# A two-block network in float32: how the second block's weights get their low parts, and how the FFN's products are grouped

## The chip, the cores and the metric

The kernel runs on one core of a Trainium2 chip. The metric is the device time of one execution in microseconds, as the median of the runs. One execution of the kernel before was profiled; all rows below are from it.

## The reference

Two blocks follow each other on 256 positions of 1024 features, all in float32. The first block has two layers, each a mixer (a chunked recurrence, then attention) and a convolutional FFN. The second block has two layers of its own. Cut to what the change touches:

```python
def conv_ffn(x, norm_g, w_up, conv_w, conv_b, w_down):      # first block, D_FF = 2816
    u = rmsnorm(x, norm_g) @ w_up
    ...                                                      # causal convolution of 3 taps
    val, gate = jnp.split(c, 2, axis=-1)
    return (jax.nn.silu(gate) * val) @ w_down

def conformer_conv(u_val, u_gate, conv_w, conv_b, ln_g, ln_b, w_pw2):
    a = u_val * jax.nn.sigmoid(u_gate)                       # the gated unit
    y = lax.conv_general_dilated(a, ...) + conv_b            # 31 taps
    y = jax.nn.silu(layernorm(y, ln_g, ln_b))
    return y @ w_pw2

def second_block(x, c, ...):
    for l in range(DEPTH):
        ...
        h = rmsnorm_2(x, g_pre[l]) * (1.0 + scale[:, None, :]) + shift[:, None, :]
        p = h @ w_in[l]
        u_val, u_gate, g_conv, c_q, c_kv, k_idx, w_idx, g_attn = jnp.split(p, offsets, axis=-1)
        y_conv = conformer_conv(u_val, u_gate, ...) * jax.nn.silu(g_conv)
        y_attn = dsa_attention(c_q, c_kv, k_idx, w_idx, ...) * jax.nn.silu(g_attn)   # scores, top-64, softmax
        y = jnp.concatenate([y_conv, y_attn], axis=-1) @ w_out[l]
        x = x + gate[:, None, :] * rmsnorm_2(y, g_post[l])
```

## The kernel before

TensorE (PE) multiplies in two ways. A plain float32 product runs as two recorded halves. A *split* product (`mm3`) writes each operand as a rounded high part plus a low part and adds three rounded products: high by high, high by low, low by high. Nearly all weights are split: SP (the sync engine's queue) loads a part of up to 1024 columns (512 KB) into a float32 page, ScalarE (ACT) copies it rounded into a page of type R (`act(hi, raw)`, line 437), and VectorE (DVE) subtracts (`tt(lo, raw, hi)`, line 450). `split_w` does this, `Chunk` calls it for each part of a weight. Weights whose name is in `NATIVE` skip it and are multiplied in float32, straight from the loaded page: in each layer of the second block the last fourth of the gated unit's weights (`u3`), half of the two gates' (`w_ga1`, `w_gc1`), and the four parts of `w_out` that take the attention's output (`oa`).

Memory is a pool of pages of 1024 columns: 24 of type R, 25 of float32 (F), cut into quarters where a tile is small, and 8 PSUM banks. The order of all instructions on the five engines is set before the run by a planner: every operation has a priority, which is its place in the program as written, an assumed duration, and for transfers an assumed `tail` until they land. Each engine takes the ready operation of lowest priority for which pages are free. `pg.spread` moves a group's priorities to a given stretch of the program, so the 120 taps of the convolution (`CONV0, CONV1 = 0.8, 1.0`) and the steps of top-k.

The FFN (`ffn`) runs over 22 values of j. `up(j)` makes two blocks of 128 features by 256 positions: 8 values of k, three rounded products of 256 columns each, both blocks in one bank. ACT and DVE put the three taps on, reading the bank, and `down(j)` adds the result's product with `w_down`. In between, DVE reduces 48 tiles of `w_ada` (128 x 1024, `stt` with an accumulator), which the second block needs. The last six `down` chunks come at the end of an FFN, and in the second FFN they are ordered by quarters of the output, each of which runs through all six chunks.

A layer of the second block (`dsa_layer`) multiplies the scaled features with `w_lat` (48 products of 456 columns, 128 tokens after the other 128), normalizes, makes the index scores on 8 heads, finds the 64 highest of each row by 8 rounds of a maximum and a replacement on DVE, and then multiplies the gated unit's weights `w_u`, whose results the taps read. Queries, gates, masked softmax of 8 heads, `w_out`'s attention half, the convolution's end and `w_out`'s other half follow.

## Time and profile before

| | us |
|---|---|
| median of 3 runs | 865.4 |
| lowest, highest | 864.19, 865.57 |
| profiled execution | 863.71 |
| its span, first to last instruction | 861.9 |
| PE busy in it | 851.7 |
| DVE busy | 725.4 |
| ACT busy | 557.1 |

How to read it: the span is what the trace covers, the execution's own time is 1.8 us longer. A busy share is an average over stages that differ, so the rows below give it by stage too. The recorded length of a matmul covers its way through the array and overlaps the next one; what a product costs is the distance from its start to the next start. The granted clock of PE is 0.99 to 1.00 of full speed in every stretch shown. The first block's mixer takes the span up to about 125 us, its first FFN the stretch to 310, the attention mixer that to 430, the second FFN that to about 610, and the two layers of the second block the rest.

### The profile page before, as it was taken

What the parts mean: (1) busy time and instruction counts of PE and PEld (TensorE: products, weight loads), DVE (VectorE), ACT (ScalarE), POOL (GpSimd) and SP (SyncE); (2) the same over time, 40 slices, a digit from 0 to 9 for tenths busy, and PEclk for the clock granted to TensorE, in tenths of its full rate; (3) what the DMA queues carried; (4) which work ended last, traced back from release to release, by engine and by line L of the source; (5) the groups of instructions that cost most, each with busy time, mean ns of one, the idle gap of its engine ahead of it and who ended that gap; (6) DMA issues with size and microseconds to landing.
All of it is one profiled execution on the core that took longest, in us unless ns stands there. A gap on an engine that the chain in (4) does not pass through costs nothing.

```text
span 861.9 us, 15745 instructions
## 1 busy us (share of the span) xinstructions
PE 851.7 (99%) x5822; PEld 776.8 (90%) x5822; DVE 725.4 (84%) x1632; ACT 557.1 (65%) x1154; POOL 0.2 (0%) x4
## 2 busy tenths in 40 slices
PE   8999999999999999999999999999999999999997
PEld 7988999999999988889989999998999857998866
DVE  6766999999977699986999976675799998799895
ACT  7856587555555496774776655566952797953883
POOL 0000000000000000000000000000000000000000
PEclk9999999999999999999999999999999999999999
DMA  8995857988865353487479975632430167440201
GB/s 318 408 354 198 285 182 225 317 294 314 303 222 180 105 182 137 146 282 264 141 229 367 351 259 177 192 118 88 155 124 14 34 213 303 138 147 14 74 1 49
DMA packets 50412, 170.27 MB, mean 198 GB/s; under 512 B 5860, under 2 KB 8436, under 8 KB 50336
## 3 DMA queue, kind: packets, MB, share of 16 engines
q1 hardware_dynamic: 50192, 169.28, 56.8%
q8 instruction: 45, 0.74, 0.3%
q14 instruction: 31, 0.25, 0.1%
q10 hardware_dynamic: 144, 0.00, 0.0%
HBM read 167.89 MB, written 1.37 MB: 196 GB/s over the span
## 4 chain that ended last, share of the span: by engine, by line
PE 95%; DVE 2%; ACT 1%; DMA 1%; issue 0%; SPq 0%; DVEq 0%; ACTq 0%
PE ps L571 26%; PE ps L573 26%; PE ps L572 26%; PE ps L424 13%; PE ps L428 2%; DVE R L450 1%; DVE F L455 1%; PE ps L582 1%; DMA F<-in_x_dram 1%; ACT F L437 0%; ACT R L437 0%; DVE F L450 0%; PE ps L1247 0%; SPq L488 0%; ACT s L437 0%
## 5 line engine op out<-in xcount | busy, mean ns | idle before, releaser
L571 PE MATMUL ps<-R,R 128*128 128x256 f32 (+2 forms) x1644 | 505.0, 307 | 1.0 <-ACT R L437 1.0
L572 PE MATMUL ps<-R,R 128*128 128x256 f32 (+2 forms) x1644 | 496.4, 302 | 1.3 <-DVE R L450 1.2
L573 PE MATMUL ps<-R,R 128*128 128x256 f32 (+2 forms) x1644 | 496.0, 302 | 0.0
L450 DVE TENSOR_TENSOR R<-F,R 128x1024 fp32r<-128x1024 f32 (+4 forms) x339 | 324.1, 986 | 43.3 <-ACT R L437 31.7
L571 PEld LDWEIGHTS ps<-R,R 128*128 128x128 f32 x1644 | 314.1, 191 | 14.8 <-ACT R L437 2.2
L572 PEld LDWEIGHTS ps<-R,R 128*128 128x128 f32 x1644 | 314.1, 191 | 12.9 <-DVE R L450 2.7
L573 PEld LDWEIGHTS ps<-R,R 128*128 128x128 f32 x1644 | 313.8, 191 | 11.8 <-DVE R L450 0.6
L437 ACT ACTIVATE R<-F 128x1024 fp32r<-128x1024 f32 (+4 forms) x339 | 282.4, 864 | 32.0 <-DVE F L450 24.5
L424 PE MATMUL ps<-F,F 128*128 128x256 f32 (+6 forms) x576 | 128.0, 375 | 0.8 <-ACT F L437 0.7
L437 ACT ACTIVATE F<-ps 128x256 f32<-128x256 f32 (+4 forms) x189 | 69.5, 399 | 69.2 <-PE ps L573 39.6
L424 PEld LDWEIGHTS ps<-F,F 128*128 128x128 f32 (+2 forms) x576 | 90.9, 190 | 19.8 <-issue 8.2
L437 ACT ACTIVATE F<-ps,par 128x256 f32<-128x256 f32 (+1 forms) x84 | 42.3, 552 | 89.0 <-PE ps L573 88.7
L455 DVE SCALAR_TENSOR_TENSOR F<-ps,par,F 128x255 f32<-128x255 f32 (+1 forms) x160 | 66.1, 476 | 27.1 <-ACT F L437 26.9
L455 DVE SCALAR_TENSOR_TENSOR F<-F,par,F 128x256 f32<-128x256 f32 (+30 forms) x206 | 86.8, 466 | 1.4 <-ACT F L437 1.3
L455 DVE SCALAR_TENSOR_TENSOR F<-F,F 128x1024 f32<-128x1024 f32 (+1 forms) x53 | 60.2, 1146 | 6.7 <-ACT F L437 6.7
L437 ACT ACTIVATE F<-F 128x256 f32<-128x256 f32 (+2 forms) x112 | 43.9, 413 | 31.7 <-DVE F L455 16.0
L450 DVE TENSOR_TENSOR F<-ps,F 128x256 f32<-128x256 f32 (+2 forms) x72 | 29.7, 443 | 18.5 <-PE ps L573 16.1
L437 ACT ACTIVATE F<-F,s 128x128 f32<-128x128 f32 (+1 forms) x80 | 33.3, 444 | 3.4 <-DVE s L476 3.0
L437 ACT ACTIVATE R<-F,par 128x256 fp32r<-128x256 f32 x32 | 14.3, 504 | 30.0 <-DVE F L450 30.0
L455 DVE SCALAR_TENSOR_TENSOR F<-F,par 128x255 f32<-128x255 f32 (+14 forms) x66 | 30.8, 467 | 0.0
L1373 ACT ACT_TABLE_LOAD x23 | 29.5, 1283 | 0.4
L428 PEld LDWEIGHTS ps<-con,F 128*128 128x128 f32 (+2 forms) x158 | 19.7, 140 | 8.9 <-issue 2.8
(96 smaller groups left out, 365.2 us busy)
## 6 DMA issues: line engine op xcount, KB each, us to landing
F<-in_f_w_up_dram SPq DMA_DIRECT2D x88, 512.0 KB, 5.5
F<-in_w_ada_dram SPq DMA_DIRECT2D x48, 512.0 KB, 5.6
F<-in_f_w_down_dram SPq DMA_DIRECT2D x44, 512.0 KB, 5.4
F<-in_w_u_dram SPq DMA_DIRECT2D x16, 512.0 KB, 5.5
F<-in_w_out_dram SPq DMA_DIRECT2D x16, 512.0 KB, 3.7
F<-in_a_w_o_dram SPq DMA_DIRECT2D x8, 512.0 KB, 10.2
F<-in_a_w_out_dram SPq DMA_DIRECT2D x8, 512.0 KB, 10.2
F<-in_w_k_dram SPq DMA_DIRECT2D x8, 512.0 KB, 4.7
```

The lines of the kernel that those rows point to most:

```text
L424: pg.add("PE", dur, lambda: nc.tensor.matmul(g(out), g(lhsT), g(rhs), start=start, stop=stop, skip_group_check=not check), [lhsT, rhs], [out])
L428: pg.add("PE", 110.0, lambda: nc.tensor.transpose(g(out), g(x), g(idn)), [x, idn], [out])
L437: nc.scalar.activation(g(out), g(x), func, bias=g(bias), scale=g(scale), **kw)
L450: return pg.add("DVE", ddur(n or x.n), lambda: nc.vector.tensor_tensor(g(out), g(x), g(y), op), [x, y], [out])
L455: nc.vector.scalar_tensor_tensor(g(out), g(x), g(s), g(y), op0, op1, **kw)
L571: nc.tensor.matmul(o, g(lh), g(rh), start=start, stop=False, **kw)
L572: nc.tensor.matmul(o, g(lh), g(rl), start=False, stop=False, **kw)
L573: nc.tensor.matmul(o, g(ll), g(rh), start=False, stop=stop, **kw)
L582: nc.tensor.matmul(g(out[e * 64:e * 64 + 64, c]), g(v[s][e]), g(p[e][:, r]), start=s == 0, stop=s == 1, skip_group_check=True)
L1373: nc.scalar.preload_act_table_set(TABLE[op[1]])
```

## The change

In both FFNs, for j from 2 on (`WIDE = 2, 2`), the high and the low part of the features lie side by side in one tile of 512 columns. `mm2` multiplies the high weights with both in one product of 512 columns and the low weights with the high half in one of 256. The bank then holds two sums; ACT copies the second out and DVE adds the first, and the taps read that sum from SBUF.

In the second block no weight but `w_uv` is loaded by SP any more. `split_dma` lets GpSimd's queue (POOL) transfer the part into an R page, which rounds it, ACT writes the negative of that into a second R page, and another transfer from POOL adds the weights to it, so that the low part is left. `NATIVE` is empty: those weights are split as well, and so is the attention's output. The gated unit, the tap sums and the taps are written right behind `w_lat`, before the normalizing and the scores, and the taps' priorities begin at 0.4. The R pages become 27, the F pages 22.

```diff
-    "R": (1024, F32R, 24),
-    "F": (1024, F32, 25),
+    "R": (1024, F32R, 27),
+    "F": (1024, F32, 22),
...
+WIDE = 2, 2
...
-CONV0, CONV1 = 0.8, 1.0
+CONV0, CONV1 = 0.4, 1.0
 TOPK = (0.0, 0.3)
-NATIVE = {"oa", "u3", "w_ga1", "w_gc1"}
+NATIVE = set()
+BY_DMA = {"oa", "oc", "pw", "uq", "u0", "u1", "u2", "u3", "w_ga0", "w_ga1", "w_gc0", "w_gc1", "lat", "qi"}
+CASTTAIL, ACCTAIL = 2500.0, 4000.0
...
+    def split_dma(dram, n):
+        hi, lo = new("w", n), new("w", n)
+        dur = n * 512 / 360.0
+        pg.add("POOL", dur, lambda: nc.gpsimd.dma_start(g(hi), dram), [], [hi], tail=CASTTAIL)
+        act(lo, hi.f32, AF.Copy, scale=-1.0)
+        pg.add("POOL", dur, lambda: nc.gpsimd.dma_start(g(lo), dram, accum_op=ALU.add), [lo], [lo], tail=ACCTAIL)
+        return hi, lo
...
-        def __init__(self, dram, kc, mc, k0=0, native=False, cuts=None):
+        def __init__(self, dram, kc, mc, k0=0, name=None, cuts=None):
             self.mc, self.kp, self.k0 = mc, 1024 // mc, k0
             self.parts = []
             for k in range(k0, kc, self.kp):
                 n = min(self.kp, kc - k) * mc
+                if name in BY_DMA:
+                    self.parts.append(split_dma(dram[:, k * mc:k * mc + n], n))
+                    continue
                 raw = new("raw", n)
...
-                self.parts.append((raw, None) if native else split_w(raw, n))
+                self.parts.append((raw, None) if name in NATIVE else split_w(raw, n))
...
+    def mm2(out, lhs, both, start, stop):
+        lh, ll = lhs
+
+        def emit():
+            nc.tensor.matmul(g(out), g(lh), g(both), start=start, stop=False, skip_group_check=True)
+            nc.tensor.matmul(g(out[:, 0:256]), g(ll), g(both[:, 0:256]), start=False, stop=stop, skip_group_check=True)
+
+        pg.add("PE", 768 / 2.4 + 6, emit, [lh, ll, both], [out])
+
...
+    def gemm_sums(ch, both):
+        out = []
+        for b in range(2):
+            ps, lo, u = psum(), blk(), blk()
+            for k in range(8):
+                mm2(ps, ch.at(k, b * 128, b * 128 + 128), both[k], k == 0, k == 7)
+            act(lo, ps[:, 256:512], AF.Copy)
+            tt(u, ps[:, 0:256], lo, ALU.add)
+            out.append(u)
+        return out
...
-        xs = []
+        xs, both = [], []
...
         def up(j):
-            ps = gemm_pair(Chunk(a["f_w_up"][l * NFF + j], 8, 256), xg if j < HEAD else xs)
+            ch = Chunk(a["f_w_up"][l * NFF + j], 8, 256)
+            if j < WIDE[l]:
+                ps = gemm_pair(ch, xg if j < HEAD else xs)
+            else:
+                us = gemm_sums(ch, both)
             if j == 0:
-                xs.extend(normed(h, r, "f_norm", 8 * l))
+                for k, x in enumerate(h):
+                    t, v = blk(), new("rr")
+                    stt(t, x, pcols("f_norm", 8 * l + k), r, ALU.mult, ALU.mult)
+                    hi, lo = v[:, 0:256], v[:, 256:512]
+                    act(hi, t, AF.Copy)
+                    tt(lo, t, hi.f32, ALU.subtract)
+                    xs.append((hi, lo))
+                    both.append(v)
             cs = []
             for b in (1, 0):
-                u, f, c = half(ps, b), b * NFF + j, blk()
+                u, f, c = half(ps, b) if j < WIDE[l] else us[b], b * NFF + j, blk()
...
-        lw = Chunk(a["w_lat"][l], 8, 456)
+        lw = Chunk(a["w_lat"][l], 8, 456, 0, "lat")
...
+        cv, us, taps = [], [], []
+        zp = psum()
+        for j in range(4):
+            ps = gemm_pair(Chunk(a["w_u"][l * 4 + j], 8, 256, 0, f"u{j}"), xs)
+            th, u2, y = blk(), blk(), blk()
+            act(th, half(ps, 1), AF.Tanh, scale=0.5)
+            stt(u2, th, 1.0, half(ps, 0), ALU.add, ALU.mult)
...
+        pg.add("PE", ZDUR, tap_sums, [cwh[:, l * 128:l * 128 + 128]] + us, [zp[:, 0:S]])
...
+        for j0 in (0, 2):
+            for s in range(1, 31):
+                for j in (j0, j0 + 1):
+                    i = (l * 32 + 30 - s) * 4 + j
+                    taps.append(stt(cv[j][:, s:], us[j][:, :S - s], cwh[:, i:i + 1], cv[j][:, s:], ALU.mult, ALU.add))
+                    if s == MEAN_AT:
+                        taps.append(stt(cv[j], mp, -1.0 / 512, cv[j], ALU.mult, ALU.add))
...
-        ch = Chunk(a["w_qidx"][l], 2, 512)
+        ch = Chunk(a["w_qidx"][l], 2, 512, 0, "qi")
...
-        topk = pg.ops[t0:]
-        cv, us, taps, p0 = [], [], [], len(pg.ops)
-        zp = psum()
-        for j in range(4):
-            ps = gemm_pair(Chunk(a["w_u"][l * 4 + j], 8, 256, 0, f"u{j}" in NATIVE), xs)
...
+        topk, p0 = pg.ops[t0:], len(pg.ops)
...
-        ch = Chunk(a["w_uq"][l], 2, 1024)
+        ch = Chunk(a["w_uq"][l], 2, 1024, 0, "uq")
...
-            ps = gemm_pair(Chunk(a[nme][l * 2 + j], 8, 256, 0, f"{nme}{j}" in NATIVE), xs)
+            ps = gemm_pair(Chunk(a[nme][l * 2 + j], 8, 256, 0, f"{nme}{j}"), xs)
...
-            ch = Chunk(a["w_out_2"][l * 8 + k], 1, 1024, 0, "oa" in NATIVE)
+            ch = Chunk(a["w_out_2"][l * 8 + k], 1, 1024, 0, "oa")
...
-        ch = Chunk(a["w_pw2"][l], 4, 512, 0, "pw" in NATIVE)
+        ch = Chunk(a["w_pw2"][l], 4, 512, 0, "pw")
...
-        chs = [Chunk(a["w_out_2"][l * 8 + k], 1, 1024, 0, "oc" in NATIVE) for k in range(4)]
+        chs = [Chunk(a["w_out_2"][l * 8 + k], 1, 1024, 0, "oc") for k in range(4)]
```

In the orders below, `ps` are PSUM banks, `R` and `F` the two types of pages and `s` small columns, and a number behind a name is that of the buffer; a matmul names its bank, then the moving operand, then the weights. Lines of the code after the change stand 4 higher up to `split_dma`, so `mm` at 428 for 424 and `act` at 441 for 437, and more behind it.

PE in the first FFN, at the first block of j = 2. Before:

```order
L573 MATMUL ps_152<-R_65,R_82 128x256
L571 MATMUL ps_156<-R_84,R_85 128x256
L572 MATMUL ps_156<-R_84,R_85 128x256
L573 MATMUL ps_156<-R_84,R_69 128x256
L571 MATMUL ps_156<-R_84,R_85 128x256
L572 MATMUL ps_156<-R_68,R_85 128x256
L573 MATMUL ps_156<-R_84,R_69 128x256
L571 MATMUL ps_156<-R_84,R_85 128x256
```

Now:

```order
L590 MATMUL ps_152<-R_81,R_76 128x256
L601 MATMUL ps_156<-R_87,R_72 128x512
L602 MATMUL ps_156<-R_87,R_75 128x256
L601 MATMUL ps_156<-R_87,R_72 128x512
L602 MATMUL ps_156<-R_87,R_75 128x256
L601 MATMUL ps_156<-R_66,R_72 128x512
L602 MATMUL ps_156<-R_66,R_75 128x256
L601 MATMUL ps_156<-R_66,R_72 128x512
```

Three products of 256 columns for each k and 128 positions of weights have become one of 512 (line 601) and one of 256 (line 602).

ACT at the start of the second block's first layer, between the scaled features of the first 128 tokens (`mod`, then a copy into R of shape 2x128) and those of the second. Before:

```order
L437 ACTIVATE F_109<-ps_152,mod_167 128x128 x2
L437 ACTIVATE R_82<-F_109 128x2x128
L437 ACTIVATE R_79<-F_93 128x1024
L437 ACTIVATE R_80<-F_105 128x1024
L437 ACTIVATE s_144<-s_145,s_139 128x1
L437 ACTIVATE s_146<-s_144 128x1
L437 ACTIVATE R_78<-F_100 128x1024
L437 ACTIVATE R_71<-F_92 128x1024
L437 ACTIVATE R_66<-F_96 128x1024
L437 ACTIVATE F_106<-ps_156,mod_167 128x128 x2
L437 ACTIVATE R_73<-F_106 128x2x128
```

Now:

```order
L441 ACTIVATE F_105<-ps_157,mod_167 128x128 x2
L441 ACTIVATE R_69<-F_105 128x2x128
L441 ACTIVATE R_82<-R_87 128x1024
L441 ACTIVATE R_68<-R_84 128x1024
L441 ACTIVATE s_116<-s_112,s_141 128x1
L441 ACTIVATE s_146<-s_116 128x1
L441 ACTIVATE R_70<-R_65 128x1024
L441 ACTIVATE R_81<-R_76 128x1024
L441 ACTIVATE F_97<-ps_152,mod_167 128x128 x2
L441 ACTIVATE R_73<-F_97 128x2x128
```

The large operations between the two groups of features read loaded F pages before (`w_qidx` and `w_u`); now they read R pages that a transfer from POOL has filled (four parts of `w_u`).

POOL, which moved nothing before, at the same place (line 539 is the rounding transfer, line 541 the one that adds):

```order
L539 DMA R_78<-in_w_lat_dram 128x912
L539 DMA R_71<-in_w_lat_dram 128x912
L541 DMA R_67<-in_w_lat_dram 128x912
L541 DMA R_72<-in_w_lat_dram 128x912
L541 DMA R_66<-in_w_lat_dram 128x912
L541 DMA R_74<-in_w_lat_dram 128x912
L539 DMA R_87<-in_w_u_dram 128x1024
L539 DMA R_84<-in_w_u_dram 128x1024
L539 DMA R_65<-in_w_u_dram 128x1024
L539 DMA R_76<-in_w_u_dram 128x1024
L541 DMA R_82<-in_w_u_dram 128x1024
L541 DMA R_68<-in_w_u_dram 128x1024
```

A group of parts is transferred, then as many transfers add to the pages of their low parts, in turn; before, SP loaded these parts in this order, `w_qidx` between them, each once.

DVE at top-k in the first layer, before:

```order
L485 MATCH_REPLACE F_99<-s_124,F_99 128x256
L482 MAX s_114<-F_99 128x8
L462 TENSOR_SCALAR R_71<-F_99 128x256
L485 MATCH_REPLACE F_99<-s_114,F_99 128x128
L450 TENSOR_TENSOR R_65<-F_87,R_79 128x1024
L482 MAX s_127<-F_99 128x8
L455 SCALAR_TENSOR_TENSOR F_99<-F_89,par,F_99 128x255
L485 MATCH_REPLACE F_99<-s_127,F_99 128x128
L455 SCALAR_TENSOR_TENSOR F_99<-F_89,par,F_99 128x254
```

Now:

```order
L489 MATCH_REPLACE F_99<-s_122,F_99 128x256
L489 MATCH_REPLACE F_99<-s_124,F_99 128x128
L486 MAX s_114<-F_99 128x8
L486 MAX s_128<-F_99 128x8
L489 MATCH_REPLACE F_99<-s_114,F_99 128x256
L489 MATCH_REPLACE F_99<-s_128,F_99 128x128
L466 TENSOR_SCALAR R_71<-F_99 128x256
L466 TENSOR_SCALAR F_106<-F_99 128x128
```

The subtraction of a weight (line 450 before, R of shape 128x1024) and taps no longer stand between the rounds; in the new order some taps stand ahead of the scores and the rest behind top-k.

## Rows read from the trace of the kernel before

**Rows 1.** The page: busy time by engine, transfers, and the chain by engine.

```profile
PE 851.7 (99%) x5822; PEld 776.8 (90%) x5822; DVE 725.4 (84%) x1632; ACT 557.1 (65%) x1154; POOL 0.2 (0%) x4
...
DMA packets 50412, 170.27 MB, mean 198 GB/s; under 512 B 5860, under 2 KB 8436, under 8 KB 50336
...
PE 95%; DVE 2%; ACT 1%; DMA 1%; issue 0%; SPq 0%; DVEq 0%; ACTq 0%
```

**Rows 2.** Stretches: us, busy PE, PEld, DVE, ACT, POOL, clock, DMA share, GB/s.

```profile
140.00:240.00 100.00, 100.00 (x835) 100.00 (x834) 92.77 (x147) 54.66 (x82) 0.00 (x0) 1.00 0.88 300
245.00:262.00 17.00, 17.00 (x144) 17.00 (x143) 11.81 (x18) 9.12 (x14) 0.00 (x0) 1.00 0.62 210
430.00:617.00 187.00, 187.00 (x1278) 174.01 (x1277) 148.20 (x244) 117.79 (x207) 0.00 (x0) 1.00 0.65 220
460.00:480.00 20.00, 20.00 (x147) 18.96 (x147) 19.15 (x34) 13.64 (x22) 0.00 (x0) 1.00 1.02 399
617.00:731.00 114.00, 112.92 (x704) 93.73 (x702) 105.19 (x305) 76.33 (x187) 0.00 (x0) 1.00 0.37 133
731.00:862.00 131.00, 124.13 (x778) 106.25 (x778) 112.90 (x325) 84.83 (x209) 0.00 (x0) 0.99 0.22 71
```

**Rows 3.** Instructions in time, PE: start, length, engine, line, shape; rounded products.

```profile
486.00 0.28 PE L573 MATMUL ps<-R,R 128*128 128x256 f32 x1
...
490.08 0.28 PE L571 MATMUL ps<-R,R 128*128 128x256 f32 x1
...
719.14 0.39 PE L571 MATMUL ps<-R,R 128*128 128x512 f32 x1
...
727.98 0.39 PE L571 MATMUL ps<-R,R 128*128 128x512 f32 x1
```

**Rows 4.** The same view: float32 products of weights and what follows them.

```profile
642.74 5.34 PE L424 MATMUL ps<-F,F 128*128 128x256 f32 x24
...
648.04 0.28 PE L572 MATMUL ps<-R,R 128*128 128x256 f32 x1
...
692.90 2.74 PE L424 MATMUL ps<-F,F 128*128 128x512 f32 x6
695.48 0.49 PE L428 MATMUL ps<-con,F 128*128 128x128 f32 x3
```

**Rows 5.** DVE: a group from 140 to 240, then instructions in time.

```profile
L455 DVE SCALAR_TENSOR_TENSOR F<-F,F 128x1024 f32<-128x1024 f32 x19 | 23.1, 1220 | 0.0
...
184.86 1.65 DVE L455 SCALAR_TENSOR_TENSOR F<-ps,par,F 128x255 f32<-128x255 f32 x4 [0.62 <-ACT F L437]
...
190.51 2.36 DVE L450 TENSOR_TENSOR R<-F,R 128x1024 fp32r<-128x1024 f32 x2
193.50 1.65 DVE L455 SCALAR_TENSOR_TENSOR F<-ps,par,F 128x255 f32<-128x255 f32 x4 [0.63 <-ACT F L437]
...
296.12 0.76 DVE L450 TENSOR_TENSOR F<-ps,F 128x256 f32<-128x256 f32 x2 [3.56 <-PE ps L573]
```

**Rows 6.** Groups from 617 to 731: busy, mean ns, idle before; ACT, then DVE.

```profile
L437 ACT ACTIVATE R<-F 128x1024 fp32r<-128x1024 f32 x14 | 14.7, 1062 | 0.0
...
L482 DVE MAX8 s<-F 128x8 f32<-128x256 f32 x8 | 3.3, 417 | 0.0
L485 DVE MATCH_REPLACE8 F<-s,F 128x256 f32<-128x256 f32 x8 | 3.3, 407 | 0.0
```

**Rows 7.** Transfers: the queue (packets, MB, share), the loads of `w_u`.

```profile
q1 hardware_dynamic: 50192, 169.28, 56.8%
...
L488 SPq DMA_DIRECT2D F<-in_w_u_dram x16: 327/328/437, 540.6 to 711.0; - x16
...
DMA to landing us min/median/max: 3.4/5.5/9.5
```

**Rows 8.** PE in time at the second block's start; the chain's last product.

```profile
598.45 1.95 PE L424 MATMUL ps<-F,F 128*128 128x128 f32 x16
...
610.82 1.89 PE L424 MATMUL ps<-F,F 128*128 128x256 f32 x8
...
855.88 0.13 PE ps L573
```

More of the change, by code (lines that the diff above doesn't have):

```diff
@@ L57 @@
     "r": ("R", 1, 256),
+    "rr": ("R", 2, 512),
     "rr": ("R", 2, 512),
@@ L654, in scaled @@
             out.append((hi, lo))
-        return out
-    def normed(xs, r, gname, i0):
-        out = []
-        for k, x in enumerate(xs):
-            t = blk()
-            stt(t, x, pcols(gname, i0 + k), r, ALU.mult, ALU.mult)
-            out.append(split_x(t))
         return out
@@ L1166, in dsa_layer, with tap_sums @@
                 mm_tm(lat[t][:, 0:456], xs[k], lw.at(k, 0, 456), t, k == 0, k == 7)
+        cv, us, taps = [], [], []
[5 more added lines that the diff above has]
+            stt(u2, th, 1.0, half(ps, 0), ALU.add, ALU.mult)
+            act(y, u2, AF.Identity, bias=bcen[:, l * 4 + j:l * 4 + j + 1], scale=cwh[:, (l * 32 + 30) * 4 + j:(l * 32 + 30) * 4 + j + 1])
+            cv.append(y)
+            us.append(u2)
+            us_op = pg.ops[-1]
+        zs, zm = wide(), blk()
+        def tap_sums():
+            for j in range(4):
+                w = g(cwh[:, l * 128:l * 128 + 128]).rearrange("p (s j) -> p s j", j=4)[:, :, j]
+                nc.tensor.matmul(g(zp[32 * j:32 * j + 32, 0:S]), w, g(us[j]), start=True, stop=True, tile_position=(0, 32 * j))
+        pg.add("PE", ZDUR, tap_sums, [cwh[:, l * 128:l * 128 + 128]] + us, [zp[:, 0:S]])
+        pg.after(memset(zs[:, 0:30], 0.0), us_op)
+        pg.after(memset(zs[:, 286:287], 0.0), us_op)
+        act(zs[:, 30:286], zp[:, 0:S], AF.Copy)
+        pg.add("SP", 200.0, lambda: nc.sync.dma_start(g(zscr), g(zs[:, 0:287])), [zs[:, 0:287]], [zscr], tail=2000.0)
+        pg.add("SP", 400.0, lambda: nc.sync.dma_start(g(zm), bass.AP(
+            tensor=g(zscr).tensor, offset=g(zscr).offset, ap=[[32 * 287, 4], [288, 32], [1, S]])), [zscr], [zm], tail=ZTAIL)
+        mp = psum()[:, 0:S]
+        mm(mp, ones, zm, True, True)
+        for j0 in (0, 2):
[5 more added lines that the diff above has]
+                        taps.append(stt(cv[j], mp, -1.0 / 512, cv[j], ALU.mult, ALU.add))
         for t in range(2):
```

28 lines of the change are left out of this document (removed).

## Prediction

> **What bounds the kernel now.** I read the page's busy shares and its chain first, then the busy time by stage, then single instructions in order of time. TensorE (PE) is busy 851.7 of 861.9 us and holds 95% of the chain [rows 1]. By stage it has no idle time at all in the FFNs, 1.1 us in the first layer of the second block and 6.9 us in the second, of which 6 us are the end, after the last product at 855.9 [rows 2, 8]. So a gain must come out of PE's own work, and it stays only as long as no other engine, nor the transfers, becomes later than PE. VectorE (DVE) is the nearest: 92.8 of 100 us in the first FFN, 105.2 of 114 in the first layer of the second block [rows 2]. The transfers have room there, share 0.37 and 0.22, because before many weights were fetched far ahead: the first load of `w_u` leaves at 540.6, its first product (float32, among those with `w_lat`) stands at 610.82 [rows 2, 7, 8].
>
> **The wide products of the FFN.** In a row of rounded products with 256 columns, 34 starts lie between 486.00 and 490.08, 0.120 us each; with 512 columns 39 starts lie between 719.14 and 727.98, 0.227 us each [rows 3]. Twice the columns costs 0.107 us more, so 0.013 us belongs to the instruction and not to its columns. Three products of 256 take 0.360 us. One of 512 and one of 256 take 0.347. The change makes 16 such pairs for each of 20 values of j in each of 2 FFNs, 640 in all: 640 x 0.013 = 8.3 us less on PE. The Trainium skill, page "TensorE: Matmul & The Clock Gate", section "Wait — 56ns, not 53.3ns?", gives a warm matmul its columns at 2.4 GHz plus a fixed 2.5 ns. By that rule the edit would save 640 x 2.5 ns = 1.6 us and the sum would end 6.7 us higher; the trace has 120 ns where the rule has 109, so it does not bear it out [rows 3].
>
> The edit adds two ACT copies and two DVE additions from PSUM per j. Such an addition costs DVE 0.34 us from start to start (two in 0.76, the second 0.42 long) [rows 5], so 0.68 per j; that the taps now read SBUF is worth nothing I can read. DVE's period is 8.64 us (184.86 to 193.50) with 0.62 us idle, so it works 8.02 us [rows 5]. PE's period shrinks by 16 x 0.013 = 0.21 to 8.43. With unchanged contents DVE would need 8.70, 0.27 too much. But this stretch holds 19 of the `w_ada` reductions in 11.6 periods, 1.64 per j, at 1.22 us [rows 5], while later in the FFN there are none (DVE 11.8 of 17 us from 245 to 262, [rows 2]). In the new order they stand thinner, about 1.3 per j and for more values of j. That takes 0.4 off: 8.3 us, just under 8.43. I cost it at nothing; if that cover fails, 40 x 0.27 = 11 us.
>
> **Float32 products become three rounded ones.** 24 recorded halves of 256 columns run from 642.74 to the start of the next rounded product but one at 648.04; less one rounded product of 0.12 that is 5.18 us for 12 products, 0.432 us each. Six halves of 512 columns take 692.90 to 695.48, 0.860 us per product [rows 4]. Replaced by 0.360 and 0.681 this gives 0.072 and 0.179. The first layer has 48 products of 256 and 16 of 512 (3.5 + 2.9 us), the second 56 and 12 (4.0 + 2.1): 12.5 us. All of it is PE's own work, in stages where PE never stands, so it counts whole if the weights are there in time.
>
> **Where the low weight parts come from.** 33 parts per layer go through GpSimd's queue (POOL), twice each. DVE loses 23 subtractions per layer at 1.14 us (two in 2.36, the second 1.22 long [rows 5]): 26 us of 105. It gains four of 0.34 for the attention output, which is now split. ACT gains 10 negations of about 1.0 us and four small copies: 76.3 becomes some 88 of 105 us, no bound [rows 2, 6]. The old kernel has no transfer from POOL (0.2 us busy; 169.3 of 170.3 MB go by one hardware queue) [rows 1, 7], so their price is bounded. A part of 512 KB moves in 1.31 us at 399 GB/s, where the engines are full (share 1.02) [rows 2]. A rounding transfer carries the same bytes: 1.31. An accumulating one also reads the page that it adds to: 1.31 if that read is hidden, 2.62 if it counts in full; less is excluded, since the bytes are the same. Nearest is the plain load, but the second read is real, so I take the middle, 1.97. 66 parts then ask 66 x 3.28 = 216 us of the engines. The window: rounded pages come free when the second FFN's last six chunks begin, 36 products of 0.227 before 598.45, at about 590; the last part must be there about 11 us (48 x 0.227) before PE's end, 6 us before the span's end, so at about 825 in a span of 842. That is 235 us, and 66 parts fit as long as an accumulating transfer costs under 235 / 66 - 1.31 = 2.25 us. At 1.97 they fit, at 92% load; PE waits for none by this sum.
>
> **The new wait.** ACT's negation waits for the rounding transfer, on an engine that works in order. At the start of a layer four negations of `w_u` stand ahead of the scaled features of the second 128 tokens, and the products with `w_lat` wait for those. Before, the same place held roundings of weights long loaded. The pages for those four come free only in the last quarter of the FFN's end (18 products, 4.1 us); a loaded part of `w_u` lands 3.4 to 9.5 us after its issue, 5.5 in the middle [rows 7]. On POOL, too, the next roundings stand behind accumulations that wait for ACT. So ACT stands 0 to 5 us, and I take 2 us at each of the two layer starts, 4 us, near the middle of the landings.
>
> **What is moved.** The gated unit (192 rounded products, 23 us) now stands right behind `w_lat`, so scores and top-k come later, and between the last score and the first masked logits PE has 138 rounded products and two float32 ones of 512, 18 us, where it had 180 and 27 float32 ones, some 33. Top-k is 8 rounds of 0.42 + 0.41 us on 256 columns and cheaper ones on 128 [rows 6]: under 13.2 us, and in the new order nothing stands between its rounds. It fits, so the move costs nothing; the taps that run early fill DVE. If DVE were still late here, each us would be PE's. The tap sums' transfers on SP no longer stand behind weight loads. More rounded and fewer float32 pages (27 and 22) leave the start's order almost as it is: nothing.
>
> **Sum.** The profiled execution took 863.7 us. 863.7 - 8.3 - 12.5 + 4.0 = 846.9. It lay 1.7 us under the median of the three runs, so I forecast 848.6 for a median.
>
> **Rivals.** (A) The transfers become the bound, and the kernel gets slower. If the page's own read counts in full, 66 x (1.31 + 2.62) = 259 us do not fit into 235; PE waits 24 us, in the stretches of the gated unit and the gates: 846.9 + 24 = 871, 872.6 as a median. It decides from 2.25 us on. For it: the early fetching from 540 on falls away, and shares of 1.02 show that the engines can be filled. Against it: the read comes from SBUF, whose port the plain loads only write. At the 300 GB/s of the first FFN instead of 399 it would be far more, which the range leaves out. The Trainium skill, page "Collectives: The Full Stack", section "The bandwidth ceiling: the fold count and why AG ≠ RS ≠ AR", states this rule: an add in the transfer engines needs two source reads on one ring and runs at half the rate of a copy. That is the 2.62; no run here shows it yet.
> (B) The wide products give nothing, since DVE is late in the FFNs or the 0.013 us stays: without the 8.3 us 856.9, with half of the 11 us 862. For it: DVE's margin is 0.1 us per j.
> (C) PE waits in many small pieces in the second block, since a part now passes transfer, ACT and transfer, where before it passed one load and two engines, with 27 pages in all. At 0.2 us per part, 66 x 0.2 = 13 us: 862.
>
> **How the numbers follow.** Forecast (842 to 853) 0.50; B 0.12; C 0.12; A 0.22; something worse 0.04. Under 0.2% (1.7 us) a measurement of this kernel can't be told from no change. B and C lie on the faster side but for their upper ends (0.05 on no change): faster 0.69, same 0.05, slower 0.26. The range runs from 841, where ACT's new wait costs nothing and a few of today's PE gaps close too, to 876, past A with its peak rate.
>
> **What would show it.** Right: in the FFNs pairs of starts 0.227 and 0.120 apart and a period of about 8.43 us; no idle PE there; no float32 product of weights; DVE near 80 us in a layer; accumulating transfers landing fast enough that PE's idle time in the second block stays under 12 us. Wrong: rows in which PE waits for transfers or for ACT's negations, a transfer share near 1 throughout the second block (A), many short waits before the first product of a part (C), or DVE over 97% busy with PE waiting for its additions (B).

## The result, and the profile after the change

| | before | after |
|---|---|---|
| median, us | 865.49 (4 runs, 864.19 to 866.33) | 916.38 (4 runs, 912.75 to 920.06) |
| profiled execution, its span | 863.71, 861.9 | 915.9, 914.1 |
| PE busy, idle | 851.7, 10.2 | 857.9, 56.2 |

The ratio is 1.0596 (95% interval 1.0574 to 1.0617): slower, where I forecast 848.6 with 0.69 on faster, and outside my range (841 to 876). The lines of the page that answer to [rows 1], with the slices of PE, its clock and the transfers, are these:

```profile
PE 857.9 (94%) x5314; PEld 761.0 (83%) x5314; DVE 706.0 (77%) x1674; ACT 603.0 (66%) x1258; POOL 93.9 (10%) x136
...
PE   9999999999999999999999999998568987968997
...
PEclk9999999999999999999999999999769998987999
DMA  8976847888877453872759850799959899996981
...
q1 hardware_dynamic: 40688, 135.13, 42.7%
q0 software_dynamic: 19008, 68.30, 31.3%
...
PE 73%; DMA 9%; issue 7%; ACT 4%; DVE 3%; POOL 3%; SPq 0%; POOLq 0%; DVEq 0%; ACTq 0%
```

PE is full through slice 27 (to about 617 us) and broken from there on; its clock falls in the emptiest of these slices or right behind them. The new queue q0 (POOL's) moves 68.3 MB in 31.3% of the span, 286 us of all sixteen engines, and transfers enter the chain with 9%. Now four stretches: one where only rounding transfers run, one where only adding ones run, and the two layers (columns as in rows 2):

```profile
598.00:602.00 4.00, 4.00 (x20) 3.40 (x19) 2.12 (x5) 3.90 (x11) 0.53 (x1) 1.00 1.13 417
609.00:615.00 6.00, 6.00 (x37) 5.62 (x36) 1.74 (x5) 3.26 (x14) 0.05 (x1) 1.00 1.06 210
...
612.00:740.00 128.00, 103.12 (x693) 91.21 (x692) 78.83 (x260) 73.91 (x165) 35.43 (x50) 0.88 0.90 221
740.00:911.00 171.00, 146.36 (x937) 129.54 (x935) 104.57 (x341) 107.15 (x260) 44.68 (x62) 0.93 0.84 200
```

The engines are full in both short stretches, at 417 and at 210 GB/s. A part of 512 KB therefore costs 1.26 us to round and 2.50 us to add. What PE waited for most, in the whole span (us in total, times, longest):

```profile
PE ps L428 <- DMA F<-zscr: 15.9, 2, 11.6
PE ps L1230 <- DVE F L459: 10.0, 2, 6.1
PE ps L428 <- DVE F L465: 6.3, 2, 3.7
PE ps L588 <- ACT R L441: 4.2, 5, 2.3
PE ps L590 <- DMA R<-in_w_ga_dram: 3.8, 2, 2.6
PE ps L590 <- DMA R<-in_w_u_dram: 3.7, 2, 2.5
```

And the group of ACT's negations (busy, mean ns, idle before them and what ended it):

```profile
L441 ACT ACTIVATE R<-R 128x1024 fp32r<-128x1024 f32 x58 | 60.2, 1056 | 55.0 <-DMA R<-in_w_qidx_dram 14.4 <-DMA R<-in_w_ga_dram 13.7 <-DMA R<-in_w_u_dram 12.0
```

Only 7.5 of these us are waits for weights (line 590, whose products read the low parts). The largest share, 25.9 us, is the tap sums (line 1230) and their round trip through memory (`zscr`), and that begins with ACT, which stood 55 us in front of its negations. The 6.3 us of line 428 behind DVE stand at the start of the second layer (760 and 772 us). One chain of tap sums in time, first ACT, then PE:

```profile
626.70 0.36 ACT L441 ACTIVATE F<-ps 128x256 f32<-128x256 f32 x1
636.64 1.06 ACT L441 ACTIVATE R<-R 128x1024 fp32r<-128x1024 f32 x1 [9.57 <-DMA R<-in_w_qidx_dram]
637.60 0.59 ACT L441 ACTIVATE F<-F,bcen,par 128x256 f32<-128x256 f32 x1
```

```profile
647.18 1.07 PE L1230 MATMUL ps<-F,par 128*32 128x256 f32 x2 [3.94 <-DVE F L459]
...
652.20 0.42 PE L589 MATMUL ps<-R,R 128*128 128x256 f32 x1
652.42 0.41 PE L590 MATMUL ps<-R,R 128*128 128x256 f32 x1
...
657.01 2.23 PE L428 MATMUL ps<-F,F 64*128 64x128 f32 x20
670.82 1.22 PE L428 MATMUL ps<-F,con 128*128 128x256 f32 x2 [11.58 <-DMA F<-zscr]
```

ACT's next work on the gated unit (637.60) stands behind the negation of `w_qidx`, and that waits 9.57 us for a rounding transfer that lies behind four adding ones of `w_u`. DVE, which stands 6.58 us for this ACT operation, then has taps ahead of the last gated result (646.71), so PE's tap sums (647.18) are late, so the small transfers through memory start late. The way to memory lands after 6.5 and 7.4 us in the two layers, where it took 2.1 before (us, min, median and max, now and before):

```profile
DMA to landing us min/median/max: 6.5/6.9/7.4
DMA to landing us min/median/max: 2.1/2.1/2.1
```

The way back takes 15.6 us here, from its issue at 655.2 to the product that reads it at 670.82, with the engines full (share 1.07). PE stands 11.58 us in front of this mean product. After such gaps it runs at the lower of its two levels, 1.2 GHz: 652.20 to 652.42 is 0.22 us per product, where [rows 3] have 0.12, and the granted clock is 0.50 in this stretch (columns as in rows 2):

```profile
650.00:655.00 5.00, 3.39 (x16) 3.40 (x17) 4.10 (x11) 1.50 (x3) 0.76 (x1) 0.50 1.11 375
```

### The profile page after: what moved, and what is told of

It reads as the page before. It is cut to its first block, busy times and chain, and to the rows that moved or that the text cites. A ratio compares the mean times of both kernels' runs of the same rounds, so it can differ in the third digit from the quotient of the medians.

```text
span 914.1 us, 14917 instructions
## 1 busy us (share of the span) xinstructions
PE 857.9 (94%) x5314; PEld 761.0 (83%) x5314; DVE 706.0 (77%) x1674; ACT 603.0 (66%) x1258; POOL 93.9 (10%) x136
## 3 DMA queue, kind: packets, MB, share of 16 engines
q0 software_dynamic: 19008, 68.30, 31.3%
## 4 chain that ended last, share of the span: by engine, by line
PE 73%; DMA 9%; issue 7%; ACT 4%; DVE 3%; POOL 3%; SPq 0%; POOLq 0%; DVEq 0%; ACTq 0%
PE ps L601 15%; PE ps L589 14%; PE ps L588 14%; PE ps L590 14%; PE ps L602 8%; PE ps L428 5%; DMA R<-in_w_out_dram 2%; DMA F<-zscr 2%; POOL R L541 2%; PE ps L432 2%; ACT F L441 2%; DVE F L459 2%; ACT R L441 2%; POOL R L539 1%; DVE R L454 1%
## 5 line engine op out<-in xcount | busy, mean ns | idle before, releaser
L588 PE MATMUL ps<-R,R 128*128 128x256 f32 (+3 forms) x1136 | 369.8, 326 | 4.2 <-ACT R L441 4.2
L590 PE MATMUL ps<-R,R 128*128 128x256 f32 (+3 forms) x1136 | 359.6, 317 | 7.5 <-DMA R<-in_w_ga_dram 3.8
L589 PE MATMUL ps<-R,R 128*128 128x256 f32 (+3 forms) x1136 | 360.7, 318 | 1.4 <-DVE R L454 1.3
L454 DVE TENSOR_TENSOR R<-F,R 128x1024 fp32r<-128x1024 f32 (+3 forms) x301 | 276.6, 938 | 30.9 <-ACT R L441 29.7
L441 ACT ACTIVATE R<-F 128x1024 fp32r<-128x1024 f32 (+3 forms) x301 | 241.2, 825 | 16.6 <-DVE F L454 13.8
L601 PE MATMUL ps<-R,R 128*128 128x512 f32 x640 | 227.8, 399 | 0.0
L602 PE MATMUL ps<-R,R 128*128 128x256 f32 x640 | 179.7, 281 | 0.0
L459 DVE SCALAR_TENSOR_TENSOR F<-F,par,F 128x255 f32<-128x255 f32 (+23 forms) x248 | 111.6, 473 | 12.0 <-ACT F L441 11.3
L441 ACT ACTIVATE R<-R 128x1024 fp32r<-128x1024 f32 (+1 forms) x66 | 67.8, 1044 | 56.9 <-DMA R<-in_w_qidx_dram 14.4
L459 DVE SCALAR_TENSOR_TENSOR F<-F,par 128x255 f32<-128x255 f32 (+20 forms) x184 | 82.1, 470 | 4.7 <-ACT F L441 4.3
L441 ACT ACTIVATE F<-F,par 128x256 f32<-128x256 f32 x96 | 57.1, 596 | 10.3 <-DVE F L454 9.0
L428 PE MATMUL ps<-F,F 128*128 128x128 f32 (+6 forms) x292 | 56.2, 357 | 6.3 <-DVE F L465 6.3
```

The source lines that it names most:

```text
L428: pg.add("PE", dur, lambda: nc.tensor.matmul(g(out), g(lhsT), g(rhs), start=start, stop=stop, skip_group_check=not check), [lhsT, rhs], [out])
L441: nc.scalar.activation(g(out), g(x), func, bias=g(bias), scale=g(scale), **kw)
L454: return pg.add("DVE", ddur(n or x.n), lambda: nc.vector.tensor_tensor(g(out), g(x), g(y), op), [x, y], [out])
L459: nc.vector.scalar_tensor_tensor(g(out), g(x), g(s), g(y), op0, op1, **kw)
L588: nc.tensor.matmul(o, g(lh), g(rh), start=start, stop=False, **kw)
L589: nc.tensor.matmul(o, g(lh), g(rl), start=False, stop=False, **kw)
```

## The experiments

Three theories stood at first: PRICE (the adding transfer's half rate fills the engines), CHAIN (transfer, ACT, transfer, on engines that work in order), ORDER (the gated unit's new place). Ratios are to the kernel before, run beside each of them; a number in brackets is the 95% interval.

**e1: the same order, no adding.**

```diff
-dma_start(g(lo), dram, accum_op=ALU.add)
+dma_start(g(lo), dram)
```

> The changed kernel, with one word less: the second transfer of each part writes the weights over the negated page instead of adding to it (so the low part is not the low part). Every instruction, its order and every wait stay; only the reading of the page by the transfer goes. Three theories. PRICE: an adding transfer moves at half the rate (in the changed kernel's trace 205 GB/s between 609 and 615 us where only such run, 414 between 598 and 602 where only rounding ones run, so 2.56 against 1.27 us for 512 KB), and 66 x 3.83 = 253 us fill the engines. Then this run asks only 132 x 1.27 = 168 us, the transfer share in the second block falls from 0.9 to about 0.6, and of the 66 x 1.29 = 85 us saved about half comes back in time: 865 to 885 us. CHAIN: what costs is the row transfer, ACT, transfer with engines in order and the tap sums' round trip behind them, not capacity. Then the landings get 1.3 us shorter and the rest stands: 900 to 916. ORDER: the gated unit's new place costs the time; 905 to 916.

882.14 us, ratio 1.0209 (1.019 to 1.0228): 34 us off, with every instruction in its place, inside PRICE's range and far from the other two. ACT's idle time before negations falls from 55.0 to 23.6 us:

```profile
L441 ACT ACTIVATE R<-R 128x1024 fp32r<-128x1024 f32 x58 | 60.2, 1055 | 23.6 <-DMA R<-in_w_out_dram 5.9 <-DMA R<-in_w_u_dram 4.7 <-DMA R<-in_w_ga_dram 4.6
```

**e2: no wait for the rounding transfer.**

```diff
-        act(lo, hi.f32, AF.Copy, scale=-1.0)
+        for c in range(0, n, 512):
+            act(lo[:, c:min(c + 512, n)], con[:, 0:min(512, n - c)], AF.Copy, scale=0.0)
```

> The changed kernel, but ACT writes the page that the second transfer adds to from a constant (two operations of 512 columns, the same ACT time), so that nobody waits for the rounding transfer before the adding one may go (the low part is left out: it becomes the whole weight). The two transfers of each part keep their price. PRICE: 253 us of engines stay; the first transfer leaves at about 571, so the last lands at 571 + 253 at the earliest, plus holes: 880 to 910 us, with a transfer share of 0.95 or more throughout the second block. CHAIN: without the wait of ACT for a transfer the taps, the tap sums and the adding transfers go early: 855 to 875. ORDER: 900 to 916.

901.04 us, 1.0424 (1.0387 to 1.046): 15 us off, within what PRICE allows and above CHAIN's 855 to 875. PE still waits 16.8 us for the tap sums' transfer. ACT's wait is a part of it, not the whole.

**e3: no transfers from POOL**; SP, ACT and DVE make the parts.

```diff
-BY_DMA = {"oa", "oc", "pw", "uq", "u0", "u1", "u2", "u3", "w_ga0", "w_ga1", "w_gc0", "w_gc1", "lat", "qi"}
+BY_DMA = set()
```

> The changed kernel with no part through GpSimd's queue: SP loads, ACT rounds and DVE subtracts as before the change, but no product of weights in float32, the gated unit and the taps early, the wide products, 27 and 22 pages. PRICE and CHAIN alike: PE is full again in the second block, with DVE nearer (26 us of subtractions more per layer): 852 to 864 us, against 865 for the kernel before. ORDER: above 880, with PE waiting for the tap sums as now.

884.88 us, 1.0231 (1.0209 to 1.0254). I had expected the kernel before, or better. By its time this spoke for ORDER; but PE waits here 19.9 us for ACT in front of line 432, and not for the tap sums, as ORDER had it.

**e4: the two transfers only for what was float32.**

```diff
+BY_DMA = {"oa", "u3", "w_ga1", "w_gc1"}
```

> The changed kernel with the two transfers only for the weights that were float32 products before (oa, u3, w_ga1, w_gc1: 20 parts in both layers); the other 46 parts are loaded by SP and split by ACT and DVE. PRICE: 20 x 3.83 + 46 x 1.3 = 137 us of the engines in a window of 235, no bound, and DVE is relieved of 20 subtractions against the run without such transfers: 848 to 858 us. CHAIN: each of the 20 still makes ACT stand in order for a transfer; 860 to 880. ORDER: above 880.

876.85 us, 1.0119 (1.0073 to 1.0165), single runs between 868.7 and 877.5. Neither PRICE nor ORDER gave this; CHAIN's 860 to 880 did.

**e5 and e6: parts of the change alone.** To the kernel before, first only the diff's lines on `WIDE`, `mm2` and `gemm_sums`; then only its order and pages, written as the changed kernel with these values:

```diff
-WIDE = 2, 2
+WIDE = 22, 22
...
-NATIVE = set()
-BY_DMA = {"oa", "oc", "pw", "uq", "u0", "u1", "u2", "u3", "w_ga0", "w_ga1", "w_gc0", "w_gc1", "lat", "qi"}
+NATIVE = {"oa", "u3", "w_ga1", "w_gc1"}
+BY_DMA = set()
```

> The kernel before, with the wide products of the FFN for j from 2 on and nothing else. By the term of my prediction (0.013 us per pair) it is 8.3 us faster: 857. By the changed kernel's trace a pair takes 0.354 us (0.237 + 0.117, between 151.76 and 157.29) and not 0.347, so 640 x 0.006 = 3.8 us less, of which 1.25 us of PE waiting in the first FFN go off; there the second block starts 2.7 us earlier than before: 862 to 863.5.

863.71 us, 0.9989 (0.9978 to 0.9999): 1.0 us by the ratio, less than either figure. Compared at the same granted clock over the span it is nearer to 2: at 0.998 four runs have 862.0 us in the mean, against 863.7 before, and at 0.994 864.5 against 866.6.

> The kernel before, with the gated unit, tap sums and taps written right behind w_lat, CONV0 = 0.4 and 27 and 22 pages, and nothing else: weights by SP, four of them float32 products, no wide products. ORDER (what made the run without POOL transfers 20 us slower than the kernel before is the new place): 870 to 885, with PE waiting for softmax steps of ACT and DVE between the heads, as there (19.9 us). The rival, DVE LOAD (it was the subtractions of the weights that were float32 before, 20 x 1.14 = 23 us more on DVE, and the order is harmless as I forecast): 864 to 867.

867.31 us, 1.0036 (1.0023 to 1.0049): 3.1 us slower. So ORDER falls, and what is left for e3 is DVE's load, with 20 subtractions of 1.14 us in both layers that the kernel before spares it. This is read from the trace; no run changed that load alone. In a stretch of e3 (columns as in rows 2) DVE is full while PE stands:

```profile
700.00:720.00 20.00, 15.90 (x59) 11.16 (x59) 20.00 (x46) 13.57 (x28) 0.00 (x0) 0.80 0.51 176
```

**e7 and e8: only the former float32 weights by POOL, in the old order**, without and with the wide products. To the kernel before:

```diff
+                if native:
+                    self.parts.append(split_dma(dram[:, k * mc:k * mc + n], n))
+                    continue
...
-            mix[4 + hp] = (None, None, t) if "oa" in NATIVE else split_x(t)
+            mix[4 + hp] = split_x(t)
```

> The kernel before in its own order and with its own pages, where only the 20 parts that are multiplied in float32 come by the rounding and the adding transfer and are multiplied in three rounded products. PRICE: the transfers ask 20 x 3.83 = 77 us, spread over two layers with a transfer share of 0.22 to 0.37, so they are hidden, and DVE gains only eight small subtractions: the 12.5 us of the float32 term come in full, 853 to 856. CHAIN: ACT stands in order for each of the 20 transfers, 3 to 9 us each, and PE behind it: 860 to 875.

> The same with the wide products of the FFN as well. By PRICE and the measured gain of the wide products 2 to 4 us less than without them: 849 to 854. By CHAIN as the run without them, less the same: 857 to 873.

879.16 us (1.0174, 1.0158 to 1.019) and 897.14 us (1.0386, 1.0363 to 1.0408). Both contradict PRICE, and both lie above CHAIN's ranges too: the transfer share is only 0.62 and 0.54 from 612 to 740 (e7's fullest stretch, 655 to 680, has 0.90), and still 15 and 33 us are lost. In e8, ACT stands 21 us in one piece for DVE, and PE 19.2 of them, while the transfer share is 0.31 (680 to 706). Full transfer engines don't explain that. The subtraction that ACT waits for stands behind taps on DVE:

```profile
691.42 10.49 DVE L457 SCALAR_TENSOR_TENSOR F<-F,par,F 128x239 f32<-128x239 f32 x28
701.82 1.23 DVE L452 TENSOR_TENSOR R<-F,R 128x1024 fp32r<-128x1024 f32 x1
...
703.08 0.87 ACT L439 ACTIVATE F<-ps 128x512 f32<-128x512 f32 x2 [20.98 <-DVE R L452]
```

The order on DVE, then, doesn't fit what happens. One thing is common to all kernels up to here that use POOL: of a part of 1024 columns the planner counts 1.46 us of moving (`dur` in the diff) and then 2.5 us until a rounding transfer lands or 4 until an adding one does, so 3.96 and 5.46 us from the issue. In the changed kernel the fastest do land so, but in the middle it is 9.8 and 7.6 (rows of line 539 and of line 541):

```profile
DMA to landing us min/median/max: 3.8/9.8/15.0
DMA to landing us min/median/max: 5.4/7.6/12.4
```

**e9: what is left without low parts.** No negation, no second transfer:

```diff
-        return hi, lo
+        return hi, hi
```

> The changed kernel without ACT's negation and without the second transfer: the rounded page stands for the low part too (the low part of the second block's weights is left out), so all products, the order as written, the wide products and the rounding transfers stay: 66 x 1.27 = 84 us of engines. REST OF THE SUM HOLDS (all that went wrong lies in how low parts are made): PE is full again, 847 to 856 us, at clock 1.00. REST FAILS TOO (products, order and wide products lose by themselves, as in the run without POOL transfers, 885): 865 to 885, with DVE near 20 of 20 us in most slices.

854.75 us, 0.9881 (0.9861 to 0.9901). That is the first of the two expectations: what went wrong lies in how low parts are made. (The prediction's sum without ACT's wait is 844.6; the other 10 us are told below, under the wide products and the gated unit.) In the first layer PE has 123.65 of 128 us at clock 1.00:

```profile
612.00:740.00 128.00, 123.65 (x854) 110.01 (x853) 95.94 (x315) 76.31 (x219) 18.15 (x35) 1.00 0.49 157
```

**e10 and e11: the planner's landings.** First only those of the tap sums (4 to 12 us below, and 2 to 6.5 us for the transfer into `zscr`), then all:

```diff
-ZDUR, ZTAIL = 480.0, 4000.0
+ZDUR, ZTAIL = 480.0, 12000.0
...
-CASTTAIL, ACCTAIL = 2500.0, 4000.0
+CASTTAIL, ACCTAIL = 9000.0, 7000.0
```

> The changed kernel, where the planner is told that the tap sums' two transfers land after 6.5 and 12 us instead of 2 and 4 (in the changed kernel 6.9 and 5.4 to 15.5, in the kernel before 2.1), so that it puts the mean product that needs them later in PE's order. PE stood 15.9 us for it. If these are a cost of their own: 893 to 903 us. PRICE and CHAIN: the weights that come later behind the same transfers then end these waits, since while PE stood the transfers caught up: 908 to 918.

> The changed kernel with all assumed landings as its trace has them: rounding transfers 9 us instead of 2.5, adding ones 7 instead of 4, the tap sums' 6.5 and 12. The planner then orders ACT, DVE and PE around what the queue does. PLAN (order made for landings that never come): 875 to 895. PRICE: the engines still have 253 us to do and PE still ends behind the last part: 900 to 918.

906.9 us (1.0486, 1.0463 to 1.0509) and 881.38 us (1.0191, 1.0169 to 1.0213): 9.5 and 35 us off, with the same bytes at the same price. The first lies between its two expectations, the second is PLAN's. With all landings as measured ACT waits 14.5 us instead of 55.0 and PE 3.3 instead of 15.9 for the tap sums:

```profile
L441 ACT ACTIVATE R<-R 128x1024 fp32r<-128x1024 f32 x58 | 60.3, 1051 | 14.5 <-DMA R<-in_w_gc_dram 7.4 <-DMA R<-in_w_uq_dram 6.6 <-DMA R<-in_w_ga_dram 0.5
```

The engines have hardly a hole left in the first layer, share 1.04 instead of 0.90 (the landings in this run are 11.2 and 9.6 us in the middle):

```profile
612.00:740.00 128.00, 113.97 (x773) 100.64 (x771) 86.12 (x285) 88.12 (x204) 45.19 (x63) 0.96 1.04 260
```

**e13: both taken away**, landings as measured, and a second transfer that doesn't add.

> The kernel with the landings as measured, and with a second transfer that writes instead of adding (the low part is not the low part); order and instructions are those of the run with the landings as measured. TWO COSTS: price and order come off one after the other, and little is left over the run with the high part alone (854.8): 850 to 862 us. ONE COST (a plan that fits hides the transfers whatever their price, and short transfers forgive a wrong plan): 872 to 881.

869.16 us, 1.0056 (1.0039 to 1.0073), between the two expectations. ACT waits for no rounding transfer any more. Alone each takes off 34 to 35 us, together 47 of the 51: some 22 us are shared, so each does part of the other's work; short transfers forgive a wrong plan, and a fitting plan hides part of long ones.

**e12, e14 and e15: versions that could be faster.** e12 is e5 with `WIDE = 22, 2`. e14 is the changed kernel with the lines below, e15 the same with `BY_DMA = {"oa"}`; the planner is also told 2.56 us for an adding transfer.

```diff
+WIDE = 22, 2
+NATIVE = {"u3", "w_ga1", "w_gc1"}
+BY_DMA = {"oa", "oc", "pw"}
+CASTTAIL, ACCTAIL = 4000.0, 5500.0
```

> The kernel before, with the wide products in the second FFN alone. There no w_ada reductions press on DVE, and with both FFNs wide the second block starts earlier by what the second FFN gave. By the 0.354 us per pair 320 x 0.006 = 1.9 us less: 861.5 to 863.5 where the kernel before has 864 to 865.4. If the wide products give nothing there either: 864 to 866.

> The changed kernel's order with the wide products in the second FFN alone, and the two transfers only for w_out and w_pw2 (20 parts in both layers, behind which the heads' work lies); the float32 products of u3, w_ga1 and w_gc1 stay, all else is loaded by SP and split. The planner is told 4 and 5.5 us of landing and 2.56 us for an adding transfer. 20 x 3.83 = 77 us of engines in two layers are no bound; PE saves the float32 products of the attention's half of w_out, 28 halves of 512 columns: 14 x 0.179 x 2 = 5.0 us by rows 4, and DVE 12 subtractions per two layers. PRICE with a fitting plan: 858 to 862. CHAIN (each wait of ACT for a transfer costs, however few): 866 to 880.

> The same with the two transfers for the attention's half of w_out alone (8 parts in both layers). PRICE: 859 to 863. CHAIN: 865 to 872.

862.69 us (0.9975, 0.9964 to 0.9986), 864.32 (0.9995, 0.9985 to 1.0004) and 863.14 (0.9985, 0.9973 to 0.9997). (On record I called the products of `w_out` halves; they are 28 products at 0.179 us.) The first has the lowest ratio of the kernels that compute everything, 0.25% under the kernel before, but the intervals of the other three such versions, e5, e14 and e15, overlap with its own. The other two lie above PRICE's ranges (e15 by 0.1 us) and below CHAIN's: they cost nothing any more, where e7 with as many parts as e14 lost 15 us. Their planned landings, 5.46 us for rounding and 8.06 for adding, are nearer to those of their traces (7.6 and 7.1 in the middle in e14, 5.4 and 5.4 in e15), and ACT waits for none. But they kept the float32 products of `u3`, `w_ga1` and `w_gc1`; so this doesn't separate the landings told to the planner from the choice of the weights.

## Why the prediction was wrong, point by point

Two steps of the sum failed: that 66 parts fit into the window, so that PE waits for none, and that ACT's new wait costs 4 us. The second rested on an order that was planned for landings which the transfers didn't keep.

**The price of the adding transfer** was mis-sized. I put 1.97 us, the middle between a plain load and one with a second read in full, and wrote that rival A decides from 2.25 us on. It measured 2.50. So 66 parts ask 66 x (1.26 + 2.50) = 248 us, more than the 235 of the prediction's window and not 92% of it. (The window opened earlier than forecast, with the first rounding transfer at 571.8 and not about 590, but that leaves next to no room either.) The upper bound of the two stood in the prediction, with its mechanism; taking the middle was the error. Without the adding the kernel is 34 us faster (e1). The Trainium skill, page "Collectives: The Full Stack", section "The bandwidth ceiling: the fold count and why AG ≠ RS ≠ AR", has the add of a collective at half the rate of a copy; 210 against 417 GB/s here agrees. With a plan that knows the landings the time is 881 (e11), 9 us above A's 872.6; but PE's waits for weights are only 3.4 us there, so a time near A's doesn't show A's waits.

**The assumed landings** were missed altogether. Raising them, with those of the tap sums, took off 35 us by itself and 13 on top of the price (e11, e13). With `dur` and `CASTTAIL, ACCTAIL = 2500.0, 4000.0` the planner lets a part land 3.96 us (rounding) and 5.46 us (adding) after its issue. The fastest landed after 3.8 and 5.4, so these numbers fit a transfer that has the engines to itself; in the middle it was 9.8 and 7.6. The Trainium skill, page "DMA: Bandwidth & Descriptors", section "Anatomy of one DMA — SWDGE (gpsimd) path", fits 2.0 us plus the bytes at 436 GB/s to a single transfer from this queue, an estimate of 3.2 us here; the fastest of this trace took 3.8. In [rows 7] plain loads of `w_u` land after 3.4 us at best and 5.5 in the middle. The prediction quoted that spread in the paragraph on ACT's wait and used it for that wait alone, not for the order that was made without it. The gap by itself need not cost: the kernel before plans 3.46 us (1.46 and 2.0) for such a load, and PE waits for none there. In the changed kernel ACT's next work for PE stood right behind the landing (637.60 above).

**ACT's new wait** I costed at 4 us, at the two layer starts only. ACT stood 55 us over the second block, in 20 pieces. I argued that queued work behind a negation was the scaled features; it was the gated unit too, and behind it the taps, the tap sums and the round trip through `zscr`. That the tap sums' transfers "no longer stand behind weight loads" was wrong in substance: they passed SP's queue freely, and the first of them then landed after 6.9 us in the middle instead of 2.1, with a transfer share of 1.07 to 1.10 where it was 0.20 before. Rival C (many small waits before the first product of a part) didn't come about: PE's waits for weights are 7.5 us, the large ones are elsewhere.

**PE's clock** was in no term. The run without low parts (e9) has the same products as the changed kernel and 839.2 us of PE's work, the changed kernel 857.9. So of the 60.7 us between their spans, 42 are idle time and 18.7 are products that take longer. Up to 612 us the two are alike (608.4 and 608.9 us of work); behind that the granted clock is 0.88 and 0.93 in the two layers, and 1.00 in e9.

**Float32 products**: right. From 865.5 the wide products alone take 1.0 and the order alone adds 3.1, which gives 867.6; without the low parts' making 854.8 were left, 12.8 less, where I had 12.5. This is a difference of three runs, and e9 also spares DVE subtractions and ACT its negations. PE's own work agrees: it is 850.7 us with the wide products alone and 839.2 in e9, 11.5 less.

**The wide products**: mis-sized. In the changed kernel a pair takes this:

```profile
151.76 0.40 PE L601 MATMUL ps<-R,R 128*128 128x512 f32 x1
152.00 0.28 PE L602 MATMUL ps<-R,R 128*128 128x256 f32 x1
152.11 0.40 PE L601 MATMUL ps<-R,R 128*128 128x512 f32 x1
...
157.29 0.28 PE L602 MATMUL ps<-R,R 128*128 128x256 f32 x1
157.41 0.28 PE L588 MATMUL ps<-R,R 128*128 128x256 f32 x1
```

Sixteen pairs in 5.65 us are 0.353 each, not 0.347: in this mix the product of 512 columns takes 0.236 and not the 0.227 of [rows 3], which came from a row of nothing but 512. So 640 pairs give some 4 us, not 8.3, and measured alone they give 1.0, or 2 at the same granted clock. Where the rest went isn't settled: PE stands 0.4 us in the first FFN and 0.3 in the second there. The rule of the Trainium skill that I set beside it (page "TensorE: Matmul & The Clock Gate", section "Wait — 56ns, not 53.3ns?": 2.5 ns per product, by my estimate 1.6 us in all) came nearer to the outcome than my term, though it gives the pair 0.325 us and the trace 0.353. DVE's cover held: it is busy 94.3 of the 100 us from 140 to 240, where it had 92.8, and PE doesn't wait there.

**The moved gated unit**, costed at nothing, costs 3.1 us alone (e6).

**What stays open.** With landings as measured and no adding, 14 us are left above e9: ACT's 66 negations and 84 us more of transfers, not separated. Nor is it settled why the old order with 20 parts by POOL loses 15 us (e7) and 18 more with the wide products (e8); the landings there (6.6 and 6.0 us in the middle in e7) exceed the planned 3.96 and 5.46 too, but a run of that order with them corrected wasn't made. The step from e7 to e8 also shows how much the planner's orders differ among themselves: 18 us for an edit that alone is worth 1 or 2. Only one other setting of the landings was tried, so how many of the 35 us belong to the landings and how many to the luck of one order isn't shown; for the landings speaks that ACT's and PE's waits fell where they should. And in e11 the planner still counts 1.46 us of moving for an adding transfer that takes 2.50; a kernel with that corrected as well wasn't run with all parts.

## What to carry to other kernels

Where a planner fixes the order from assumed durations, compare each assumed landing and price with the nearest measured one under load before anything else: here the constants fitted a transfer on idle engines, and raising those of the parts and of the tap sums together took off 35 of 51 us. A transfer that adds should be costed at its upper bound until a row shows otherwise, and a transfer share that comes out near 0.9 is best taken as a bound: here a small transfer on another queue, of the kind that PE waits for, already took 8.1 and 5.8 us in the middle instead of 2.1 in e1 and e13, whose shares over the layers are 0.67 to 0.84. When work is taken from the engine that sets the time, the next one must have the room: DVE without POOL's help (e3) seems not to have had it.

## What the runs showed that I had not expected

A rounding transfer is not slower than a plain load (417 GB/s, [rows 2] have 399), and an adding one runs at almost exactly half of it (210). POOL's instruction that issues a transfer took 0.53 us in the middle when all transfers were plain and 0.87 when adding ones were in the queue, the plain ones of that queue included (e1 and the changed kernel, with the same order). A transfer of 128 KB on SP's queue took up to 15.6 us, from its issue to the product that read it, while POOL's queue kept the engines full. A product of 512 columns took 0.236 us between products of 256, and 0.227 among its like.
